# Routing stage of a two-layer decoder step: which engine splits the expert tiles, how many are issued per routing step, and where the softmax exponentials stand

## The chip, the cores and the metric

The kernel runs on one core of a Trainium2 chip. A core has TensorE (PE, matrix products; PEld is its weight load), VectorE (DVE), ScalarE (ACT), GpSimd (POOL) and SyncE (SP, which issues most transfers). Each engine works through its own instructions strictly in order and waits for others only by semaphores. The metric is the device time of one execution in microseconds (us), lower is better.

## The reference, cut to what matters

Two layers; in each, three token mixers are merged, then a PEER expert mixer follows. Only the expert mixer matters here:

```
q  = (x @ p_wq).reshape(T, 8 heads, 2 halves, 128)
sc = einsum('thjc,hjkc->thjk', q, p_keys)            # 128 keys in each half
s, i  = top_k(sc, 16)
cand  = s[:,:,0,:,None] + s[:,:,1,None,:]            # 16 x 16 sums
cidx  = i[:,:,0,:,None]*128 + i[:,:,1,None,:]
top_s, pos = top_k(cand.reshape(T, 8, 256), 16)
eidx  = take_along_axis(cidx, pos);  g = softmax(top_s)
act   = gelu(u[eidx] . x) * g
out   = sum_k act[k] * v[eidx[k]]                    # 16384 experts
```

There are 256 prompt tokens and 32 sample tokens (8 sequences of 4), and 1024 channels.

## The kernel before, in words

For the prompt tokens the kernel does not gather experts. It multiplies all 16384 rows of `u` with the tokens, as 128 *expert tiles* of 128 rows (`u_tile`), takes the Gelu, multiplies with gate weights that are zero for experts not chosen, and then multiplies with all of `v` (`experts`). For the 32 sample tokens it gathers rows.

All products are made from float32 values split in two: `split` writes the rounded high part with a ScalarE copy (line 209) and the low part with a subtraction (line 210) on VectorE, or on GpSimd where `eng` is given. `proj` loads a 512 KB weight tile, splits it, and issues 24 matrix products in one PSUM bank: 16 with the high weights (lines 253 and 254) and 8 with the low ones (line 256). So the low part is wanted only after the first 16. There are two such banks (`ps_pj`), three raw buffers (`NRAW`) and four buffers for the split halves (`NHI`), that is two tiles' worth.

`peer` runs a layer's expert mixer in three stages. **Routing**: the generator `routing` issues the query projections, the scores, the maxima and the index lookups, and after each of its `yield`s `peer` adds `RU[phase]` to a due count and issues one more expert tile when the count asks for it. What a `yield` yields is the phase: 0 beside the score maxima (36 yields, 16 of them ahead of the second half of the query projections), 1 beside the maxima of the candidate sums (18), 2 beside the lookups (26). **Gate weights**: `gate_weights` for 8 tokens at a time, with the remaining expert tiles between. **Experts**: the products with `v`.

In the routing, one call of `top16` is a chain of five VectorE operations (maximum of 8, index, replace, maximum of 8, index). Tokens come in three segments `s` of 128, 128 and 32. In phase 2, each segment begins with its softmax (subtraction of the maximum, `Exp` on ScalarE, sum, reciprocal, product), then index arithmetic, then for each of two words the lookups `eq`, `eq`, `res` in pairs of heads. Then PE turns the results and the digits of the keys go to `pd`, `pu` and `pg`, which the gate weights read.

In the mixers and in the experts stage, the order of each engine's instructions is the program's. In the routing and the gate stage it is not: a scheduler orders them when the program is built. It plays out a timeline with its own durations, and puts next on an engine the instruction that is earliest in the program among those it takes as ready. That order is then fixed. When an operation takes longer on the chip than in that timeline, everything behind it on its engine waits. `Exp` and `Gelu` are in different function tables of ScalarE, so each change between them loads a table.

The routing's temporary tiles (`tk`) and the second part of the Gelu outputs (`WB`, 28 KB per partition) take the same memory one after the other, and the tiles of the gate stage (`gw`) lie behind `WB`.

Of the kernel before, what the change touches and what calls it, by code (L numbers as in the profile page):

```python
# [7 lines left out]
F32 = mybir.dt.float32  # L8
# [7 lines left out]
AF = mybir.ActivationFunctionType  # L16
OP = mybir.AluOpType
AX = mybir.AxisListType
# [4 lines left out]
TP = 256  # L23
# [21 lines left out]
NGB = 4  # L45
XPRE = (3, 7)
PEX = 6
RU = (0.25, 0.5, 1.05)

GS = 2.0 ** 15  # L50
RATE = (24, 30, 18, 6, 24, 14, 12)
# [14 lines left out]
def bc(ap, shape):  # L66
    return ap.to_broadcast(shape)


class Kernel:  # L70
# [1223 lines left out]
    def peer(self):  # L1294
        tc = self.tc
        with tc.tile_pool(name="pk", bufs=1) as self.pk:
            with tc.tile_pool(name="wa", bufs=1) as wa:
# [3 lines left out]
                with tc.tile_pool(name="tk", bufs=1) as self.tk:  # L1301
                    due = 0.0
                    for self.phase in self.routing():
                        due += RU[self.phase]
                        if self.jdone < min(J1, int(due)):
# [32 lines left out]
    def routing(self):  # L1338
        ve, ac, sy, pe, L, I, tk = self.ve, self.ac, self.sy, self.pe, self.L, self.I, self.tk
# [3 lines left out]
        def top16(src, n, v, i, w):  # L1343
            ve.max(v[:, 0:8], src)
            ve.max_index(i[:, 0:8], v[:, 0:8], src)
            tmp = tk.tile([128, w], F32, tag="tmp", name="tmp", bufs=2)
            ve.match_replace(tmp, v[:, 0:8], src, -3.0e38)  # L1347
            ve.max(v[:, 8:16], tmp)
            ve.max_index(i[:, 8:16], v[:, 8:16], tmp)

        pss = self.ps_rc("pss").rearrange("p (m k) -> p m k", k=128)
        for grp in range(2):
# [5 lines left out]
            for t in range(2):  # L1358
                for half in range(2):
                    p = self.ps_rc("psc").rearrange("p (m k) -> p m k", k=128)  # L1360
# [4 lines left out]
            for s2 in range(2):  # L1365
                s = 2 * grp + s2
# [3 lines left out]
            for t, half, p in banks:  # L1370
                for m in range(4):
                    h, j = divmod(8 * grp + 4 * half + m, 2)
# [6 lines left out]
        picks = []  # L1379
        for s in range(3):  # L1380
            H = 8 if s < 2 else 2
            v, ix = val[s], idx[s]
            cand = tk.tile([128, H, 80], F32, tag="cand", name="cand")
            s0, s1 = v[:, :, 0], v[:, :, 1]
            a0 = 0
            for g, (na, nbb) in enumerate(((1, 16), (1, 16), (2, 8), (4, 4), (8, 2))):
                ve.tensor_tensor(cand[:, :, 16 * g:16 * g + 16].rearrange("p h (a b) -> p h a b", b=nbb),  # L1387
                                 bc(s0[:, :, a0:a0 + na].unsqueeze(3), [128, H, na, nbb]),
                                 bc(s1[:, :, None, 0:nbb], [128, H, na, nbb]), op=OP.add)
                a0 += na  # L1390
            top = tk.tile([128, H, 16], F32, name=f"top{s}")
            pos = tk.tile([128, H, 16], U32, name=f"pos{s}")
            for h in range(H):
                top16(cand[:, h], 128, top[:, h], pos[:, h], 80)
                yield 1
            picks.append((top, pos))
        for s in range(3):
            H, ix = 8 if s < 2 else 2, idx[s]

            (tops, pos), top = picks[s], tk.tile([128, H, 16], F32, tag="tope", name="tope")  # L1400
            ve.tensor_tensor(top, tops, bc(tops[:, :, 0:1], [128, H, 16]), op=OP.subtract)
            ac.activation(top, top, AF.Exp)
            z = tk.tile([128, H], F32, tag="z", name="z")
            ve.tensor_reduce(z, top, axis=AX.X, op=OP.add)
            ve.reciprocal(z, z)
            gd = self.sg if s == 2 else top
            ve.tensor_tensor(gd.rearrange("p (h r) -> p h r", r=16) if s == 2 else gd, top,
                             bc(z.unsqueeze(2), [128, H, 16]), op=OP.mult)
            yield 2

            it = lambda n: tk.tile([128, H, 16], I32, tag="it", name=n, bufs=5)
            p32 = pos.bitcast(I32)
            gq, r = it("gq"), it("r")
            ve.tensor_scalar(gq, p32, 4, None, op0=OP.logical_shift_right)
            ve.tensor_scalar(r, p32, 15, None, op0=OP.bitwise_and)
            sh = it("sh")
            ve.tensor_scalar(sh, gq, -1.0, 5.0, op0=OP.mult, op1=OP.add)
            t1 = it("t1")
            ve.tensor_tensor(t1, r, sh, op=OP.logical_shift_right)
            t2 = it("t2")  # L1420
            ve.tensor_tensor(t2, t1, sh, op=OP.logical_shift_left)
            bq = r
            ve.tensor_tensor(bq, r, t2, op=OP.subtract)
            ve.tensor_tensor(t2, bc(self.one_i[:, 0:1].unsqueeze(2), [128, H, 16]), gq, op=OP.logical_shift_left)
            ve.tensor_scalar(t2, t2, 1, None, op0=OP.logical_shift_right)
            aq = t1
            ve.tensor_tensor(aq, t1, t2, op=OP.add)
            yield 2
            out = []
            for w_, place in ((0, aq), (1, bq)):  # L1430
                pf = tk.tile([128, H, 16], BF16, tag="pf", name="pf")
                ve.tensor_copy(pf, place)
                kf = tk.tile([128, H, 16], BF16, tag="kf", name="kf")
                ve.tensor_copy(kf, ix[:, :, w_])
                res = tk.tile([128, H, 16], F32, tag=f"res{w_}", name=f"res{w_}")
                for h0 in range(0, H, 2):
                    eq = tk.tile([128, 2, 16, 16], BF16, tag="eq", name="eq", bufs=2)
                    ve.tensor_tensor(eq, bc(pf[:, h0:h0 + 2].unsqueeze(3), [128, 2, 16, 16]),
                                     bc(self.iota16[:, None, None, :], [128, 2, 16, 16]), op=OP.is_equal)
                    ve.tensor_tensor(eq, eq, bc(kf[:, h0:h0 + 2].unsqueeze(2), [128, 2, 16, 16]), op=OP.mult)  # L1440
                    ve.tensor_reduce(res[:, h0:h0 + 2], eq, axis=AX.X, op=OP.add)
                    yield 2
                out.append(res)
            if s < 2:
                tt = slice(s * 128, (s + 1) * 128)
                keys = tk.tile([128, 2, 128], F32, tag="keys", name="keys")
                ki = tk.tile([128, 2, 128], I32, tag="ki", name="ki")
                for src, dst, scale in ((out[0], keys[:, 0], 1.0), (out[1], keys[:, 1], 1.0), (top, self.pg[:, 0, tt], GS)):
                    pt = self.ps_rc("ptk")[:, :128]
                    pe.transpose(pt, src.rearrange("p h r -> p (h r)"), self.ident)  # L1450
                    ac.activation(dst, pt, AF.Copy, scale=scale)
                ve.scalar_tensor_tensor(self.pg[:, 1, tt], pt, GS, self.pg[:, 0, tt], op0=OP.mult, op1=OP.subtract)
                ve.tensor_copy(ki, keys)
                ve.tensor_scalar(ki, ki, 15, None, op0=OP.bitwise_and)
                ve.tensor_copy(self.pu[:, :, tt], ki)
                ve.tensor_tensor(self.pd[:, :, tt], keys, self.pu[:, :, tt], op=OP.subtract)
                yield 2
            else:
                f = lambda x: x.rearrange("p h r -> p (h r)")
                for dst, hi, lo in ((self.se, out[0], out[1]), (self.sv, out[1], out[0])):  # L1460
                    ve.scalar_tensor_tensor(dst, f(hi), 128.0, f(lo), op0=OP.mult, op1=OP.add)
                    if L:
                        ve.tensor_scalar(dst, dst, float(L * 16384), None, op0=OP.add)


    def u_tile(self):
        ac, j, t = self.ac, self.jdone, self.tdone
        self.jdone += 1
        ps = self.proj(self.I["ut"][self.L, j], "pu", TP, self.gp if self.phase in (0, 1) else None)
        w = self.slot(j)  # L1470
        if t < TP:
            ac.activation(w[:, t:], ps[:, t:], AF.Gelu)  # L1472
        if t:
            ge = self.gw.tile([128, TP], F32, tag="ge", name="ge", bufs=2)
            ac.activation(ge[:, :t], ps[:, :t], AF.Gelu)
            self.ve.tensor_tensor(w[:, :t], w[:, :t], ge[:, :t], op=OP.mult)
# [366 lines left out]
```

## Time and profile before

| | |
|---|---|
| median of 3 runs | 2542.75 us (2541.96 to 2546.72) |
| the profiled execution | 2553.09 us |
| its span, first to last instruction | 2551.3 us |
| PE busy | 2457.7 us (96%) |
| PEld busy | 2235.0 us (88%) |
| DVE busy | 1935.7 us (76%) |
| ACT busy | 1328.5 us (52%) |
| POOL busy | 269.9 us (11%) |
| granted TensorE clock, mean | 0.979 |

A row names the engine, the line of the kernel, and the tiles as written<-read. "Idle before" is what the engine stood still ahead of an instruction, with the one that released it. Instructions on VectorE and matrix products on PE overlap a little with the next, so the step from start to start is shorter than the duration. The profiled execution's routing of layer 0 lies between 427 and 634 us, that of layer 1 between 1695 and 1902 us.

### The profile page before, as it was taken

To read this page: it belongs to the slowest core of one execution; us is meant where nothing else is said; L and a number is where in the kernel's file an instruction comes from. 1 tells how busy PE (TensorE), PEld (TensorE's weight loads), DVE (VectorE), ACT (ScalarE), POOL (GpSimd) and SP (SyncE) were. 2 spreads that over 40 slices of the span, in tenths; PEclk is the share of its full clock that TensorE was granted. 3 is DMA by queue.
4 is the path that set the end of the run, shared out by engine and by line. 5 is a ranking of instruction groups with operands and counts; after the bars stand their busy time and mean duration, and the time that the engine had idled before them with its cause. 6 is when DMAs were issued, how large, how long until landed. Compare 5 with 4: busy or idle time off the path is not lost. (4 is left out here: it accounts for less than half of the span.)

```text
span 2551.3 us, 45304 instructions
## 1 busy us (share of the span) xinstructions
PE 2457.7 (96%) x17014; PEld 2235.0 (88%) x17014; DVE 1935.7 (76%) x4156; ACT 1328.5 (52%) x2675; POOL 269.9 (11%) x270
## 2 busy tenths in 40 slices
PE   8998998989999999999999999989899999999998
PEld 8987897989999988777789888889899999878886
DVE  7667666699778868888676776767997787688885
ACT  6444765445554444444564457653455544444544
POOL 0000100240000012222000001003300000122210
PEclk9999999999999999999999989999999999999999
DMA  4422543546545568888544225434455455688883
GB/s 163 136 92 82 183 143 111 166 143 190 167 163 166 162 216 304 313 305 300 167 134 137 83 88 188 146 111 163 157 183 166 161 164 165 234 308 311 311 281 132
DMA packets 132028, 465.10 MB, mean 182 GB/s; under 512 B 15360, under 2 KB 17536, under 8 KB 131808
## 3 DMA queue, kind: packets, MB, share of 16 engines
q1 hardware_dynamic: 109728, 385.14, 45.4%
q0 software_dynamic: 22080, 77.06, 9.0%
q8 instruction: 134, 2.20, 0.3%
q14 instruction: 86, 0.70, 0.1%
HBM read 451.32 MB, written 10.82 MB: 181 GB/s over the span
## 5 line engine op out<-in xcount | busy, mean ns | idle before, releaser
L210 DVE TENSOR_TENSOR hl<-raw,hl 128x1024 fp32r<-128x1024 f32 (+1 forms) x842 | 844.8, 1008 | 393.3 <-ACT hl L209 382.5
L209 ACT ACTIVATE hl<-raw 128x1024 fp32r<-128x1024 f32 (+1 forms) x880 | 778.2, 888 | 461.4 <-PE pu L254 144.6
L1555 PE MATMUL acc<-hl,wh 128*128 128x512 f32 x2048 | 648.3, 396 | 2.6 <-ACT hl L209 1.4
L253 PE MATMUL pu<-hh,hl 128*128 128x256 f32 x2048 | 504.5, 287 | 12.4 <-ACT WA L1472 12.2
L254 PE MATMUL pu<-hl 128*128 128x256 f32 x2048 | 494.9, 280 | 0.0
L1555 PEld LDWEIGHTS acc<-hl,wh 128*128 128x128 f32 x2048 | 384.7, 188 | 100.5 <-ACT hl L209 4.9
L1555 PE MATMUL acc<-hl,wl 128*128 128x512 f32 x1024 | 404.9, 395 | 0.0
L253 PEld LDWEIGHTS pu<-hh,hl 128*128 128x128 f32 x2048 | 388.2, 190 | 14.1 <-ACT WA L1472 13.3
L254 PEld LDWEIGHTS pu<-hl 128*128 128x128 f32 x2048 | 387.8, 189 | 0.0
L326 PE MATMUL pz<-xl,hl 128*128 128x288 f32 x1008 | 325.0, 322 | 0.6 <-DVE xl L1663 0.3
L324 PE MATMUL pz<-xh,hl 128*128 128x288 f32 x1008 | 308.5, 306 | 11.8 <-ACT xh L209 6.8
L328 PE MATMUL pz<-xh,hl 128*128 128x288 f32 x1008 | 306.7, 304 | 0.0
L256 PE MATMUL pu<-hh,hl 128*128 128x256 f32 x2048 | 284.8, 282 | 2.3 <-DVE hl L210 2.3
L256 PEld LDWEIGHTS pu<-hh,hl 128*128 128x128 f32 x2048 | 260.0, 189 | 3.1 <-DVE hl L210 3.0
L1555 PEld LDWEIGHTS acc<-hl,wl 128*128 128x128 f32 x1024 | 192.5, 188 | 45.7
L209 ACT ACTIVATE wh<-WA 128x256 fp32r<-128x256 f32 x200 | 83.6, 418 | 269.1 <-PE acc L1555 266.7
L326 PEld LDWEIGHTS pz<-xl,hl 128*128 128x128 f32 x1008 | 197.4, 196 | 16.7 <-issue 11.5
L324 PEld LDWEIGHTS pz<-xh,hl 128*128 128x128 f32 x1008 | 197.6, 196 | 14.5 <-ACT xh L209 7.4
L328 PEld LDWEIGHTS pz<-xh,hl 128*128 128x128 f32 x1008 | 198.4, 197 | 3.7 <-issue 2.7
L1676 POOL DMA_INDIRECT gbuf<-in_u,se x64 | 61.7, 964 | 963.3 <-PE pu L256 701.0
L210 DVE TENSOR_TENSOR wl<-WA,wh 128x256 fp32r<-128x256 f32 x200 | 84.3, 422 | 48.4 <-ACT wh L209 48.2
L210 POOL TENSOR_TENSOR hl<-raw,hl 128x1024 fp32r<-128x1024 f32 (+1 forms) x38 | 89.6, 2357 | 188.2 <-ACT hl L209 165.6
(584 smaller groups left out, 3366.0 us busy)
## 6 DMA issues: line engine op xcount, KB each, us to landing
raw<-in_ut SPq DMA_DIRECT2D x256, 512.0 KB, 3.5
raw<-in_v SPq DMA_DIRECT2D x256, 512.0 KB, 4.7
raw<-in_win SPq DMA_DIRECT2D x126, 512.0 KB, 3.6
raw<-in_wq SPq DMA_DIRECT2D x32, 512.0 KB, 3.5
raw<-in_wbr SPq DMA_DIRECT2D x24, 512.0 KB, 3.5
raw<-in_wout SPq DMA_DIRECT2D x16, 512.0 KB, 3.6
CS<-in_C SPq DMA_DIRECT2D x16, 256.0 KB, 3.9
out_sC<-CS POOLq DMA_DIRECT2D x16, 256.0 KB, 2.8
```

What stands on the lines that cost most here:

```text
L209: self.ac.activation(hi, r, AF.Copy)
L210: (eng or self.ve).tensor_tensor(lo, r, hi.bitcast(F32), op=OP.subtract)
L253: self.pe.matmul(ps, wh[k], self.xh[:, k, :n], start=(k == 0), stop=False)
L254: self.pe.matmul(ps, wh[k], self.xl[:, k, :n], start=False, stop=False)
L256: self.pe.matmul(ps, wl[k], self.xh[:, k, :n], start=False, stop=(k == 7))
L324: self.pe.matmul(ps, hi[:, m], xh, start=(first and m == 0), stop=False)
L326: self.pe.matmul(ps, hi[:, m], xl, start=False, stop=False)
L328: self.pe.matmul(ps, lo[:, m], xh, start=False, stop=last)
L1555: pe.matmul(acc[t][d], lhs[:, 128 * t:128 * t + 128], rhs, start=False, stop=last and n == 2, skip_group_check=True)
L1676: self.gp.indirect_dma_start(out=g, out_offset=None, in_=src, in_offset=bass.IndirectOffsetOnAxis(ap=ix[:, r:r + 1], axis=0))
```

## The change

Three things are changed. The rates `RU` at which expert tiles are issued: more in phase 0, the same in phase 1, fewer in phase 2. The engine of the low parts' subtraction for expert tiles: GpSimd in phase 0 alone, where it was phases 0 and 1. The softmax: the subtraction stands with the candidate maxima (phase 1), for each segment in a tile `ex` of its own; the three `Exp` stand together after the first word's lookups of segment 0, each pinned behind what is already issued on ScalarE; the sum, the reciprocal and the product come after the segment's lookups. The `yield 2` behind the old softmax is gone, so phase 2 has 23 yields.

```diff
-RU = (0.25, 0.5, 1.05)
+RU = (0.42, 0.5, 0.9)
...
-            picks.append((top, pos))
+            ex = tk.tile([128, H, 16], F32, name=f"ex{s}")
+            ve.tensor_tensor(ex, top, bc(top[:, :, 0:1], [128, H, 16]), op=OP.subtract)
+            picks.append((pos, ex))
         for s in range(3):
             H, ix = 8 if s < 2 else 2, idx[s]
-
-            (tops, pos), top = picks[s], tk.tile([128, H, 16], F32, tag="tope", name="tope")
-            ve.tensor_tensor(top, tops, bc(tops[:, :, 0:1], [128, H, 16]), op=OP.subtract)
-            ac.activation(top, top, AF.Exp)
-            z = tk.tile([128, H], F32, tag="z", name="z")
-            ve.tensor_reduce(z, top, axis=AX.X, op=OP.add)
-            ve.reciprocal(z, z)
-            gd = self.sg if s == 2 else top
-            ve.tensor_tensor(gd.rearrange("p (h r) -> p h r", r=16) if s == 2 else gd, top,
-                             bc(z.unsqueeze(2), [128, H, 16]), op=OP.mult)
-            yield 2
+            pos, top = picks[s]
...
                 out.append(res)
+
+                if s == w_ == 0:
+                    for _, ex in picks:
+                        self.tc.keep_in_program_order(ac.activation(ex, ex, AF.Exp))
+
+            z = tk.tile([128, H], F32, tag="z", name="z")
+            ve.tensor_reduce(z, top, axis=AX.X, op=OP.add)
+            ve.reciprocal(z, z)
+            gd = self.sg if s == 2 else top
+            ve.tensor_tensor(gd.rearrange("p (h r) -> p h r", r=16) if s == 2 else gd, top,
+                             bc(z.unsqueeze(2), [128, H, 16]), op=OP.mult)
...
-        ps = self.proj(self.I["ut"][self.L, j], "pu", TP, self.gp if self.phase in (0, 1) else None)
+        ps = self.proj(self.I["ut"][self.L, j], "pu", TP, self.gp if self.phase == 0 else None)
```

## Rows read from the trace of the kernel before

**Rows 1.** Page, part 1: busy us (share of the span) and instructions of each engine.
```profile
PE 2457.7 (96%) x17014; PEld 2235.0 (88%) x17014; DVE 1935.7 (76%) x4156; ACT 1328.5 (52%) x2675; POOL 269.9 (11%) x270
```
**Rows 2.** Waits of PE, 427 to 640 us: who for whom, total us, times, longest.
```profile
PE pu L253 <- ACT WA L1472: 6.1, 1, 6.1
...
PE pu L256 <- DVE hl L210: 1.0, 1, 1.0
```
**Rows 3.** Timeline of PE at the long wait, both layers: start, us, instructions [idle before].
```profile
533.77 1.11 PE L256 MATMUL pu<-hh,hl 128*128 128x256 f32 x8
...
536.58 1.11 PE L256 MATMUL pu<-hh,hl 128*128 128x256 f32 x8
543.81 0.58 PE L253 MATMUL pu<-hh,hl 128*128 128x256 f32 x1 [6.12 <-ACT WA L1472]
...
547.40 1.55 PE L256 MATMUL pu<-hh,hl 128*128 128x256 f32 x8
...
1811.48 0.58 PE L253 MATMUL pu<-hh,hl 128*128 128x256 f32 x1 [6.12 <-ACT WA L1472]
```
**Rows 4.** Timeline of ACT around the same wait, layer 0.
```profile
535.09 1.28 ACT L1402 ACT_TABLE_LOAD   x1
541.75 0.31 ACT L1402 ACTIVATE tope<-tope 128x128 f32<-128x128 f32 x1 [5.38 <-DVE tope L1401]
542.08 1.28 ACT L1472 ACT_TABLE_LOAD   x1
543.38 0.38 ACT L1472 ACTIVATE WA<-pu 128x256 f32<-128x256 f32 x1
```
**Rows 5.** Timeline of DVE: three long operations, one of usual length, the awaited subtraction.
```profile
513.60 1.95 DVE L1387 TENSOR_TENSOR cand<-val 128x128 f32<-128x128 f32 x1
...
516.15 1.79 DVE L1434 CAST kf<-idx 128x128 bf16<-128x128 uint32 x1
...
541.25 0.27 DVE L1387 TENSOR_TENSOR cand<-val 128x128 f32<-128x128 f32 x1
541.44 0.28 DVE L1401 TENSOR_TENSOR tope<-top 128x128 f32<-128x128 f32 x1
...
549.53 2.13 DVE L1425 TENSOR_SCALAR t<-t 128x128 int32<-128x128 int32 x1
```
**Rows 6.** Timeline of POOL at the same times: the expert tiles' low parts.
```profile
512.64 5.22 POOL L210 TENSOR_TENSOR hl<-raw,hl 128x1024 fp32r<-128x1024 f32 x2 [0.41 <-ACT hl L209]
...
549.08 2.50 POOL L210 TENSOR_TENSOR hl<-raw,hl 128x1024 fp32r<-128x1024 f32 x1 [1.92 <-ACT hl L209]
```
**Rows 7.** Timelines of PE and DVE at the first expert tile that DVE splits.
```profile
550.65 1.11 PE L256 MATMUL pu<-hh,hl 128*128 128x256 f32 x8
...
556.28 1.22 PE L256 MATMUL pu<-hh,hl 128*128 128x256 f32 x8
555.01 1.21 DVE L210 TENSOR_TENSOR hl<-raw,hl 128x1024 fp32r<-128x1024 f32 x1
```
**Rows 8.** Busy us (count) of PE, PEld, DVE, ACT, POOL; PE clock; DMA.
```profile
460.00:505.00 45.00, 45.00 (x359) 44.04 (x358) 30.94 (x151) 18.42 (x27) 12.07 (x6) 1.00 0.51 164
505.00:537.70 32.70, 32.69 (x281) 32.16 (x279) 32.70 (x193) 14.33 (x20) 24.40 (x10) 1.00 0.53 177
537.70:549.00 11.30, 5.19 (x26) 5.19 (x27) 11.30 (x77) 4.28 (x7) 2.38 (x1) 0.70 0.20 59
549.00:634.00 85.00, 83.88 (x717) 83.16 (x716) 82.20 (x202) 45.74 (x70) 2.50 (x1) 1.00 0.57 179
```
**Rows 9.** Groups of DVE's instructions by line, 504.9 to 634.8 us: busy, mean ns | idle.
```profile
L210 DVE TENSOR_TENSOR hl<-raw,hl 128x1024 fp32r<-128x1024 f32 x30 | 36.4, 1216 | 3.7 <-ACT hl L209 3.4 <-issue 0.3
...
L1515 DVE TENSOR_TENSOR oj<-dgd,dones 128x1024 int32<-128x1024 int32 x3 | 3.6, 1214 | 0.0
```
**Rows 10.** Timeline of DVE: first digits of the gate stage; the routing's last lookup.
```profile
599.19 0.35 DVE L1490 TENSOR_TENSOR dhi<-iota_hi,pd 128x128 f16<-128x128 f16 x2
...
632.99 0.18 DVE L1461 SCALAR_TENSOR_TENSOR se<-res,res 128x32 int32<-128x32 f32 x1
```

## The prediction

> **What bounds the kernel now.** I read the page first. PE is busy for 96% of the span and nothing else comes near [rows 1], so a saving must be time in which PE stands still or runs slowly, and work taken from another engine counts only where PE waits for it. Next, the waits of PE over the routing of layer 0: apart from the start of the stage, which the change leaves alone, there is one wait of 6.1 us for a Gelu (line 1472) and one of 1.0 us for a low half from VectorE (line 210) [rows 2]. Layer 1 has the same long wait, 6.12 us [rows 3].
>
> Then the timelines. An expert tile's last products normally end 2.81 us after those of the tile before (536.58 after 533.77, equal durations). Around the wait they end 11.26 us later (548.95 after 537.69) [rows 3]. So the wait costs 11.26 - 2.81 = 8.45 us: 6.12 of idling and some 2.2 because the tile that follows runs with products of 0.4 us each. The stretch around it has a mean granted clock of 0.70 where its neighbours have 1.00 [rows 8]: after the idle time the lower of the two levels (1.2 instead of 2.4 GHz) was granted for about one tile.
>
> Why PE waited: there are two PSUM banks for expert tiles, and ScalarE did not empty them. It had loaded the table of `Exp` at 535.09, ahead of a Gelu whose products were finished, and stood 5.38 us until VectorE had written the softmax's subtraction at 541.44 to 541.72. Only after a second table load came the Gelu, at 543.38 [rows 4, 5]. The order was fixed at build with that subtraction taken as ready by about 535; on the chip VectorE was some 6.5 us behind. It was not idle: it is busy for all of 505 to 549 [rows 8]. A good part of the delay is visible in it. Sums of candidates and casts that normally take about 0.27 us take 1.8 to 2.1 us, and end when a GpSimd subtraction ends [rows 5, 6]. There are five such operations in each layer, about 1.7 us too long each (the three shown: 1.68, 1.6, 1.9); three lie ahead of 521 us, two behind 545 us. The maxima beside them are not prolonged.
>
> **The change part by part.** *Counts.* Before: 36 x 0.25 + 18 x 0.5 + 26 x 1.05 = 45.3, so 45 expert tiles in the routing, 18 of them split by GpSimd, 4 ahead of the second query projections. After: 15.12 + 9 + 23 x 0.9 = 44.8, so 44, of which GpSimd splits 15 and 6 lie ahead of the second projections. All 128 are issued in any case, one more in the gate stage, so PE's own work stays as it is.
>
> *The exponentials.* They are now pinned behind the Gelu of tile 28 (24.12 + 5 x 0.9 = 28.6), where the old one stood ahead of that of tile 14. The 8.45 us per layer at the old place go, 16.9 us in all. What comes in their place: one table load, three exponentials and a load back, 1.28 + 0.9 + 1.30 = 3.5 us in which ScalarE does nothing else, if it need not wait. The old block ran from 535.09 to 543.38, 8.3 us, for 6.1 us of PE's idling [rows 3, 4], so some 2 us of a block are hidden by the two banks. That leaves 1.3 us per layer if they stand in one piece, 0 if a copy goes between; I take 1. The four table loads saved per layer (5.1 us of ScalarE) lie beside PE's work and are worth nothing. Bounds: -0 and +3.3, the latter if VectorE is as late with segment 2's subtraction as it is below with a split.
>
> The Trainium skill, ScalarE: Activation LUTs, section "What ACT_TABLE_LOAD costs", gives 2.66 us for a switch, a drain of 1.38 us beside the load of 1.28 us. Here the Gelu starts 1.30 us after the load does [rows 4], so no drain shows; by the page the new block would be 2.7 us longer and this term 3.7 us instead of 1.
>
> *GpSimd in phase 0 alone.* Nine tiles of phase 1 move to VectorE, and six new ones of phase 0 go to GpSimd: VectorE splits 29 instead of 27. The two blocked operations behind 545 us go (3.4 us of VectorE), the three ahead of 521 us stay (5.1 us), since they lie beside phase 0's tiles now as before. So VectorE still falls behind its planned order by 5 to 6.5 us while GpSimd splits. Before, tiles 10 to 18 did not ask VectorE for anything and PE ran on until the exponential. Now tile 16 asks it. The cover: the buffer of a low half is free when the tile two ahead has ended (551.76), and the low half is wanted 4.5 us later (556.28), of which 1.21 us is the subtraction, so VectorE may be 3.1 us late; at the first such tile of before it was just that [rows 7]. What is left is 5 to 6.5 less 3.1, 2 to 3.4 us per layer; I take 3. Bounds: 0, if the scheduler's order has room there, and 6.5, if none of the cover is left. Behind it, waits of the kind that before shows (1.0 us [rows 2]) stay: 1.3 us per layer.
>
> *Fewer tiles beside the lookups, more ahead.* With two more tiles ahead of the second projections, the second scores come 2 x 2.81 = 5.6 us later. VectorE has no work then (it idles 14 of the 45 us from 460 to 505 [rows 8]), while PE is ahead by the two tiles. From there to the last lookup, VectorE must do: busy 126.2 us from 505 to 634 [rows 8], less 28 splits of 1.21 us, 34 [rows 9], less about 8 of gate work done early (three `oj` of 1.21 us, three `oi` of half that, their digits [rows 9, 10]), less 8.6 of blocking, which is 75.6. In the new kernel: 75.6 + 5.1 + 29 x 1.21 = 116 us, from 510.6 to 626. PE needs 38 x 2.81 = 107 us for its tiles, from 512 to 619. So VectorE ends 7 us behind PE where before both ended together (last lookup at 632.99 [rows 10]). PE can pass this with tiles of the gate stage: two banks and two `ge` buffers hold four, 11 us. I cost it at nothing; without that cover it is 7 us and more (the third rival).
>
> *The small rest* (the subtraction in another tile, the sum and product later) are the same instructions; 0.
>
> *Sum.* Before, per layer: 8.45 + 1.0 = 9.4. After: 1 + 3 + 1.3 = 5.3. The gain is 4.1 per layer, 8.2 us for both. The profiled execution would go from 2553.1 to 2544.9; it is 10.3 us above the median of the runs, so I take the difference from the median: 2542.75 - 8.2 = 2534.5 us.
>
> **The rivals.** *A, the wait goes and nothing takes its place.* For it: VectorE shows little idle time but also few late splits from 560 on, though it is busy for 82.2 of 85 us [rows 8], so the fixed order can absorb a delay; and phase 0 now takes 36 maxima beside 15 tiles, at nearly PE's pace. Against it: the three blocked operations stay. It gives 16.9 to 18.8 us less: 2524 to 2526.
>
> *B, the wait moves.* The delay of VectorE, not the place of the `Exp`, is the cause; the first splits of phase 1 and the pinned exponentials inherit it. The delay is 6.5 us at least; less one cover, plus 3.5 for the block and later waits, it costs 7.5 to 9.5 per layer. It gives 2542.75 within 4 us: 2539 to 2544. For it: VectorE is full from 505 on [rows 8]. Against it: a wait in small pieces need not lower the clock (after the 1.0 us wait products have their usual length), and two of five blocks are gone.
>
> *C, slower: VectorE's tail holds the gate stage.* The place is the end of the routing. The routing's temporary tiles grow: `ex` takes 512 + 512 + 128 bytes per partition and `tope` gives back 512, which by my count brings them from 28448 to 29088 bytes, over the 28672 of `WB`, and so under the first tile of the gate stage, `dhi`. Before, the digits began at 599.19, 34 us ahead of the last lookup [rows 10]; then they must wait for the key tiles of segment 1. If the scheduler lets PE have no tile beyond the 44th meanwhile, PE stands from 619 to 626 and on through 4 to 6 us of gate work that was done early before: 12 to 13 us, with 2.3 for the other waits some 15 per layer against 9.4. That is +5 per layer: about 2553. It decides from the point at which fewer than two extra tiles are let in: each gives PE 2.81 us for 1.21 of VectorE.
>
> The Trainium skill, GPSIMD Engine Reference, section "Key points", says that GpSimd shares its SBUF interfaces with VectorE and collides with instructions of two SBUF inputs. The rows agree for the candidate sums [rows 5, 6]. No row shows a VectorE split, which also has two SBUF inputs, beside a GpSimd one; by the page tile 16's, beside tile 15's, could lose up to 2.4 us, and the sum would be 2.4 per layer worse.
>
> **How the numbers follow.** The forecast, 5 to 12 us less, 0.42; A 0.20; B 0.23; C 0.15. The time is the forecast's: 2534.5 us. The range reaches to A's 2524 and over B's 2544 to 2546; it leaves out most of C and a little below A. A change under 0.2% (5.1 us) can hardly be told from none here. Faster by more: the forecast and A, 0.62. Within: B, 0.23. Slower: C, 0.15.
>
> **What would show it.** In the new trace: no 6 us wait of PE for a Gelu near 537 and 1805 us, and a granted clock of 1.00 there; one load of the `Exp` table per layer; 15 GpSimd splits per layer; three long VectorE operations per layer and none after GpSimd stops; a wait of PE for `hl` from VectorE of 2 to 3.4 us at the first tile of phase 1; at most 1 us of waiting around the exponentials; no PE gap between routing and gate stage. The prediction is wrong if the `Exp` still stands on VectorE for over 3 us, if the waits for `hl` add up to over 6 us per layer, or if PE idles where the gate stage begins.

## The result, and the profile after

The changed kernel is slower. Its median is 2562.95 us (2557.55 to 2571.68) beside 2546.14 us for the kernel before (8 runs of each); the ratio is **1.0063, 95% interval 1.0046 to 1.0079**, or 12 to 20 us. I had forecast 2534.5 us, within 2524 to 2546: the sign was wrong. The profiled execution took 2563.68 us (span 2561.9 us, mean granted clock 0.979, as before).

The busy times (columns as in [rows 1]) say little: PE has the same work, and the span has grown beside it.

```profile
PE 2459.6 (96%) x17014; PEld 2240.3 (87%) x17014; DVE 1938.0 (76%) x4162; ACT 1314.1 (51%) x2667; POOL 250.4 (10%) x264
```

The waits of PE in the routing of layer 0, 420 to 660 us (who for whom: total us, times, longest), answer to [rows 2]. The first line stands at the first VectorE split, the second and third at the end of the routing, the last at the exponentials.

```profile
PE pu L256 <- DVE hl L210: 3.6, 1, 3.6
PE pu L253 <- ACT ge L1478: 3.4, 1, 3.4
PE pg L1527 <- DVE oj L1518: 3.2, 1, 3.2
PE pu L253 <- ACT WA L1475: 2.0, 1, 2.0
```

The single wait of 6.1 us [rows 2] is gone. Four waits of 2.0 to 3.6 us have taken its place, 12.2 us in all. In layer 1 they are `hl` 4.0, `ge` 3.4 and `WA` 2.0 us, and none for `oj`.

**The first VectorE split.** Timelines of PE and DVE (columns as in [rows 3]), layer 0:

```profile
529.13 1.11 PE L256 MATMUL pu<-hh,hl 128*128 128x256 f32 x8
535.71 2.07 PE L256 MATMUL pu<-hh,hl 128*128 128x256 f32 x8 [3.61 <-DVE hl L210]
541.00 1.30 PE L256 MATMUL pu<-hh,hl 128*128 128x256 f32 x8
...
511.55 1.96 DVE L1387 TENSOR_TENSOR cand<-val 128x128 f32<-128x128 f32 x1
514.10 2.03 DVE L1426 CAST kf<-idx 128x128 bf16<-128x128 uint32 x1
516.32 2.67 DVE L1387 TENSOR_TENSOR cand<-val 128x128 f32<-128x128 f32 x2
534.45 1.20 DVE L210 TENSOR_TENSOR hl<-raw,hl 128x1024 fp32r<-128x1024 f32 x1
```

Two tiles end at 537.78 and 542.30, 7.54 and 4.52 us after the one before them, where 2.81 is usual [rows 3]. So the wait costs 6.4 us (5.4 in layer 1), not the 3.6 us of idling: behind it the lower of the two clock levels (1.2 GHz) was granted for a while again (the mean is 0.73 in the first of the stretches below), as behind the old wait in [rows 8].

**The exponentials.** Timeline of ACT, then of PE, around them:

```profile
575.14 0.39 ACT L1475 ACTIVATE WA<-pu 128x256 f32<-128x256 f32 x1 [1.07 <-PE pu L256]
575.54 1.28 ACT L1439 ACT_TABLE_LOAD   x1
576.83 0.63 ACT L1439 ACTIVATE ex<-ex 128x128 f32<-128x128 f32 x3
577.37 1.04 ACT L209 ACTIVATE hl<-raw 128x1024 fp32r<-128x1024 f32 x1
578.32 0.25 ACT L1454 ACTIVATE keys<-ptk 128x128 f32<-128x128 f32 x1
578.59 1.28 ACT L1475 ACT_TABLE_LOAD   x1
579.88 0.38 ACT L1475 ACTIVATE WA<-pu 128x256 f32<-128x256 f32 x1
...
574.00 1.10 PE L256 MATMUL pu<-hh,hl 128*128 128x256 f32 x8
575.20 1.21 PE L256 MATMUL pu<-hh,hl 128*128 128x256 f32 x8
...
578.01 0.28 PE L254 MATMUL pu<-hl 128*128 128x256 f32 x1
580.32 0.39 PE L253 MATMUL pu<-hh,hl 128*128 128x256 f32 x1 [2.03 <-ACT WA L1475]
```

One table load for `Exp`, no wait of ACT for VectorE: this part does what it says. But PE works on two tiles in turn here, and both are finished within 1.3 us (575.10 and 576.41). The block stands between their two Gelus and takes 4.3 us, since a copy of a split and an eviction are caught between its loads. The first Gelu has emptied one bank, and PE works in it until 578.29; then it needs the other, whose Gelu is 3.5 us late, and waits 2.0 us. In layer 1 the wait is the same, but behind it the lower clock level was granted (products of 0.41 instead of 0.28 us; layer 0 kept 1.00). Columns as in [rows 8]:

```profile
1860.00:1870.00 10.00, 8.91 (x62) 8.91 (x63) 7.12 (x16) 4.65 (x7) 0.00 (x0) 0.83 0.52 160
```

**The end of the routing.** Timelines of ACT, DVE and PE. The Gelu at 621.36 is the 44th, the last that writes all 256 tokens without `ge`:

```profile
621.36 0.37 ACT L1475 ACTIVATE WA<-pu 128x256 f32<-128x256 f32 x1
627.21 0.36 ACT L1475 ACTIVATE WA<-pu 128x248 f32<-128x248 f32 x1
630.30 0.24 ACT L1478 ACTIVATE ge<-pu 128x8 f32<-128x8 f32 x2 [2.73 <-DVE pd L1459]
...
629.79 0.42 DVE L1459 TENSOR_TENSOR pd<-keys,pu 128x256 f16<-128x256 f32 x1
630.24 0.36 DVE L1493 TENSOR_TENSOR dhi<-iota_hi,pd 128x128 f16<-128x128 f16 x2
...
626.05 1.11 PE L256 MATMUL pu<-hh,hl 128*128 128x256 f32 x8
630.53 0.58 PE L253 MATMUL pu<-hh,hl 128*128 128x256 f32 x1 [3.37 <-ACT ge L1478]
...
642.79 1.08 PE L1527 MATMUL pg<-oj,oi 128*128 128x128 f16 x16 [3.15 <-DVE oj L1518]
```

Two tiles of the gate stage, the 45th and 46th, get through and fill the two banks. Their `ge` may be written only after the last key tile (`pd`, until 630.21). PE stands for it, then stands again for the first gate weights, whose digits `dhi` began behind `pd` too (before, they began at 599.19 [rows 10]). Counted from the first product of the query projections, that `pd` is done 209.8 us into the stage (211.9 in layer 1), 6.2 and 8.5 us later than before. Busy times in stretches (columns as in [rows 8]): the first split, the routing's last tiles, its end, where the clock falls too.

```profile
530.00:540.00 10.00, 6.39 (x39) 6.19 (x38) 10.00 (x64) 2.15 (x4) 0.00 (x0) 0.73 0.22 68
...
612.00:627.00 15.00, 15.00 (x130) 14.95 (x128) 13.36 (x27) 8.07 (x14) 0.00 (x0) 1.00 0.67 200
627.00:650.00 23.00, 16.32 (x145) 15.90 (x144) 21.87 (x60) 6.99 (x21) 0.00 (x0) 0.85 0.28 91
```

**Where the time went, by stage.** I measure, in each layer's timeline, the time from the first product of the query projections to the end of the Gelu of the 28th, 44th and 50th expert tile, and to the first product with `v`, and take it from that of the kernel before. Positive is ahead (us, layer 0 / layer 1; the kernel before: 159.0 / 158.7, 204.5 / 204.3, 222.8 / 222.6, 477.4 / 477.2). The kernels of the experiments are in the same table; "tiles" is how many expert tiles the routing issues.

| kernel | tiles | at 28 | at 44 | at 50 | at `v` | ratio to before (95%) |
|---|---|---|---|---|---|---|
| changed | 44 | 3.9 / 3.1 | 3.2 / 0.9 | -9.5 / -6.3 | -7.8 / -5.6 | 1.0063 (1.0046 to 1.0079) |
| e1_ex_in_qT | 44 | 3.9 / 3.7 | 1.0 / 2.4 | -5.4 / -4.0 | -4.7 / -3.3 | 1.0047 (1.0035 to 1.006) |
| e2_before_pad | 44 | -0.5 / -0.1 | 0.9 / 1.4 | 0.2 / 0.6 | 0.0 / 0.5 | 0.9993 (0.9979 to 1.0006) |
| e3_softmax_only | 41 | 1.0 / 2.4 | -0.1 / 1.4 | -0.1 / 1.6 | 1.3 / 2.8 | 0.9991 (0.9975 to 1.0007) |
| e4_rates_only | 47 | 3.9 / 3.7 | 5.4 / 5.2 | 3.3 / 3.1 | 3.7 / 3.4 | 0.998 (0.9964 to 0.9995) |
| e6_rate_up | 47 | 4.1 / 3.9 | 5.1 / 5.0 | 3.7 / 3.6 | 3.9 / 3.9 | 0.9976 (0.9958 to 0.9994) |
| e7_exp_apart | 47 | 3.5 / 3.6 | 4.0 / 4.3 | 2.5 / 2.7 | 3.0 / 3.3 | 0.9961 (0.9941 to 0.998) |
| e8_rates_pinned_adds | 47 | 8.0 / 7.6 | 5.9 / 5.6 | 7.0 / 6.7 | 6.8 / 6.5 | 0.9953 (0.9934 to 0.9971) |
| e9_rate_up_only | 47 | 4.3 / 3.7 | 5.9 / 5.4 | 7.1 / 6.6 | 3.1 / 2.6 | 0.9976 (0.9961 to 0.9991) |
| e10_apart_pinned | 47 | 7.5 / 7.5 | 5.6 / 5.7 | 5.6 / 5.7 | 5.7 / 5.9 | 0.9957 (0.994 to 0.9974) |

The changed kernel is ahead up to the 44th tile, by somewhat less than I had summed, and loses 12.7 and 7.2 us between the 44th and the 50th. A part of these two numbers is order: 65 and 49 of the gate weights' products stand there, 29 in the kernel before, and 16 of them take about 1 us. The two layers' -7.8 and -5.6 make 13.4 us, inside the measured 12 to 20. The last two columns agree within the interval for every kernel but e1 (8.0 us by the stage, 9 to 15 by the ratio), so the stage explains the time.

What was open was the cause at the end of the routing: the grown temporary tiles, which put the first gate tiles behind `pd`; the number of tiles PE has left when VectorE finishes; or the softmax itself.

### The profile page after: what moved, and what is told of

Read it like the earlier page. It is cut to its first block, busy times and chain, and to the rows that moved or that the text cites. A ratio compares the mean times of both kernels' runs of the same rounds, so it can differ in the third digit from the quotient of the medians.

```text
span 2561.9 us, 45294 instructions
## 1 busy us (share of the span) xinstructions
PE 2459.6 (96%) x17014; PEld 2240.3 (87%) x17014; DVE 1938.0 (76%) x4162; ACT 1314.1 (51%) x2667; POOL 250.4 (10%) x264
## 5 line engine op out<-in xcount | busy, mean ns | idle before, releaser
L210 POOL TENSOR_TENSOR hl<-raw,hl 128x1024 fp32r<-128x1024 f32 (+1 forms) x32 | 74.6, 2332 | 170.3 <-ACT hl L209 147.9
```

What stands on the lines that cost most here:

```text
L210: (eng or self.ve).tensor_tensor(lo, r, hi.bitcast(F32), op=OP.subtract)
```

## The experiments

### e1_ex_in_qT: the changed kernel without the growth of its temporary tiles

```diff
         picks = []
+        exs = tk.tile([128, 18, 16], F32, tag="qT", name="ex")
...
-            ex = tk.tile([128, H, 16], F32, name=f"ex{s}")
+            ex = exs[:, 8 * s:8 * s + H]
```

> The changed kernel with one thing undone: the three ex tiles take the memory of qT, which is dead by then, so the routing's temporary tiles do not grow and the gate stage's first tiles no longer lie over key tiles. Theory M (memory): the gate stage's digits can again be written before the routing ends; the waits of PE for ge (3.4 us per layer) and oj (3.2 us) and the slow tiles behind them go. Of the 12.7 and 7.2 us that the changed kernel loses between expert tiles 44 and 50, about 10 and 6 come back: some 2 to 6 us faster than the kernel before, ratio 0.998 to 1.000. Theory V (VectorE's tail): two tiles more ahead of the second scores and fewer beside the lookups leave VectorE late whatever the memory; it stays at the changed kernel's ratio, 1.004 to 1.008.

**Measured:** 2562.19 us, ratio 1.0047 (1.0035 to 1.006). The `ge` no longer waits for `pd`, and the stage gains 3.1 and 2.3 us over the changed kernel. But it is still slower than before. VectorE now does gate work ahead of the routing's last lookups, so the last key tile comes later (645.66 instead of 629.79), and a copy on ACT into `WB`, which takes the memory of the routing's tiles, waits for it. PE still stands 2.9 us for a `ge`, in both layers. Timelines of DVE and ACT, and PE's wait:

```profile
645.66 0.43 DVE L1460 TENSOR_TENSOR pd<-keys,pu 128x256 f16<-128x256 f32 x1
...
646.18 0.73 ACT L1537 ACTIVATE WB<-pg 128x112 f32<-128x112 f32 x4 [3.13 <-DVE pd L1460]
...
PE pu L253 <- ACT ge L1479: 2.9, 1, 2.9
```

**What follows:** the memory decides what waits for VectorE's tail, not whether something does. By the stage 5.4 of 13.4 us went with the growth, and the two ratios' intervals overlap; the larger part of the loss stays.

### e2_before_pad: the kernel before with as much growth

```diff
-            z = tk.tile([128, H], F32, tag="z", name="z")
+            z = tk.tile([128, 8 + 160], F32, tag="z", name="z")[:, :H]
```

> The kernel before with 640 bytes per partition of padding in the tile z, so that the routing's tiles end where those of the changed kernel do; no work is changed. Theory M: the digits move behind the last key tile, PE waits at the start of the gate stage as in the changed kernel, and the time rises by 6 to 18 us, ratio 1.002 to 1.007. Theory V: memory plays no part, ratio 1.000 within 0.001.

**Measured:** ratio 0.9993 (0.9979 to 1.0006). The first digits begin at 624.0 instead of 599.19 [rows 10], yet the table's row is that of the kernel before within 1.4 us. **What follows:** 25 us of delay of the early gate work cost nothing where PE's routing tiles reach as far as VectorE's tail. The growth alone, without the other edits, is not the cause.

### e3_softmax_only: the new softmax with the old rates and the old use of GpSimd

The kernel is that of e1 with these two lines as before:

```diff
-RU = (0.42, 0.5, 0.9)
+RU = (0.25, 0.5, 1.05)
...
-        ps = self.proj(self.I["ut"][self.L, j], "pu", TP, self.gp if self.phase == 0 else None)
+        ps = self.proj(self.I["ut"][self.L, j], "pu", TP, self.gp if self.phase in (0, 1) else None)
```

> The kernel before with the softmax alone moved (ex in the memory of qT); the rates and GpSimd's phases are those of before. If the place of the Exp was the cause of the long wait, the 6.1 us wait and the slow tile go in both layers: 12 to 17 us faster, ratio 0.993 to 0.995. If VectorE's delay is the cause and only moves, PE waits elsewhere (first VectorE split, new Exp) for about as long: ratio 0.998 to 1.001.

**Measured:** ratio 0.9991 (0.9975 to 1.0007). The wait for the Gelu is gone, and at the first VectorE split this stands in its place (timeline of PE, layer 0; 5.1 us in layer 1):

```profile
540.12 1.11 PE L256 MATMUL pu<-hh,hl 128*128 128x256 f32 x8
550.44 2.08 PE L256 MATMUL pu<-hh,hl 128*128 128x256 f32 x8 [7.34 <-DVE hl L210]
```

**What follows:** VectorE is late, and the old `Exp` was only where PE met it. Moving the `Exp` moves the wait to the next thing that PE wants of VectorE: rival B's mechanism. This kernel issues only 41 tiles in the routing, and PE waits nowhere at its end: VectorE, with 23 splits in the routing instead of 29, is done with the last `pd` 205.5 and 203.8 us into the stage, and the gate stage's first tiles get through. So it is not the count of tiles by itself that decides, but whether PE's tiles reach as far as VectorE's tail.

### e4_rates_only: the new rates and GpSimd in phase 0 alone, the old softmax

The kernel before with the two lines of e3 the other way round. The old softmax keeps its `yield 2`, so phase 2 has 26 yields and the routing issues 47 tiles.

> The kernel before with the rates and the GpSimd phases alone changed; the softmax is the old one. The Exp of segment 0 may still be placed ahead of a Gelu, and the first VectorE split of phase 1 now meets a VectorE that is 5 to 6.5 us late. If the delay passes on to whatever asks VectorE first: a wait for hl of about 3.5 us per layer, little left for the Exp to wait, ratio 0.998 to 1.002. If both waits add: ratio 1.002 to 1.005.

**Measured:** ratio 0.998 (0.9964 to 0.9995). The 6.1 us wait is gone here too, though the `Exp` stands where it stood: ACT comes to it later and finds the subtraction done (table load at 547.20, `Exp` at 548.50, no wait). What is left is 3.6 us for `hl` and 0.6 us for `ge` in each layer. **What follows:** the rates and the engine alone make the kernel a little faster, and the end of the routing costs little (1.7 and 1.8 us of lead between the 44th tile and `v`). What the new softmax brings beside its place is three yields fewer, hence three tiles fewer.

### e6_rate_up: the kernel of e1 with 47 tiles

```diff
-RU = (0.42, 0.5, 0.9)
+RU = (0.42, 0.5, 1.03)
```

> The changed kernel with ex in the memory of qT (as in the run before, which alone gave a ratio of 1.0047) and 1.03 instead of 0.9 expert tiles per step of phase 2: 47 tiles are issued in the routing as where only the rates were changed, instead of 44. Theory T: PE runs out of routing tiles before VectorE ends its lookups, and the gate stage is held by that tail; three tiles more cover it, 4.3 us per layer come back between tiles 44 and 50: ratio 1.0005 to 1.002. Theory X: only the joint block of the exponentials costs; nothing comes back, ratio 1.0035 to 1.006.

**Measured:** 2542.29 us, ratio 0.9976 (0.9958 to 0.9994), against 1.0047 for e1: 0.71%, or 18 us, for one number. The wait for `ge` at the end of the routing and the 2.0 us at the exponentials are gone; 3.6 us for `hl` (4.0 in layer 1) and 0.4 us for `WA` stay. **What follows:** with these rates and this use of GpSimd, 44 tiles are too few, at least without the growth.

### e9_rate_up_only: the changed kernel with 47 tiles, growth and all

The same one-number edit, on the changed kernel itself.

> The changed kernel with one number altered: phase 2's rate is 1.03 instead of 0.9, so 15.1 + 9 + 23 x 1.03 = 47.8, 47 expert tiles in the routing instead of 44; the softmax and its tiles stay as changed, memory growth included. Nothing of the computation is left out. Theory S (tile supply: PE runs out of routing tiles while VectorE finishes the lookups): the loss goes although the memory grows; ratio to before 0.996 to 1.000, 2540 to 2549 us; no wait of PE for `oj` or for a late `ge` of more than 1 us, and tile 50 ends 3 us earlier than before. Theory M (the grown temporary tiles hold `dhi` and with it the gate stage): most of the loss stays; ratio 1.003 to 1.006, 2557 to 2563 us, with `dhi` still behind the last key tile and a wait of 3 us for `oj`.

**Measured:** 2543.95 us, ratio 0.9976 (0.9961 to 0.9991), where the changed kernel has 1.0063 (0.87% less, 22 us). Waits of PE in layer 0, then the end of the routing on ACT and DVE:

```profile
PE pu L256 <- DVE hl L210: 4.0, 2, 3.6
PE pg L1527 <- DVE oj L1518: 1.2, 1, 1.2
...
PE pu L253 <- ACT ge L1478: 0.3, 1, 0.3
```

```profile
624.12 0.36 ACT L1475 ACTIVATE WA<-pu 128x256 f32<-128x256 f32 x1
626.93 0.36 ACT L1475 ACTIVATE WA<-pu 128x248 f32<-128x248 f32 x1
627.19 0.17 ACT L1478 ACTIVATE ge<-pu 128x8 f32<-128x8 f32 x1
...
625.39 0.42 DVE L1459 TENSOR_TENSOR pd<-keys,pu 128x256 f16<-128x256 f32 x1
625.84 0.36 DVE L1493 TENSOR_TENSOR dhi<-iota_hi,pd 128x128 f16<-128x128 f16 x2
```

The digits still stand behind `pd`, as in the changed kernel, but the last tile without `ge` ends at 624.48, 1.3 us ahead of `pd`'s end (625.81); in the changed kernel it ends 8.5 us ahead (621.73 and 630.21), in the kernel before 0.9 us behind it (632.08 and 631.22). Three tiles are 8.4 us.

The wait at the exponentials has gone too. The higher rate shifted the pinned block by one Gelu, to behind both of a pair, so that both banks were empty and PE had work for all of its 4.2 us (timeline of ACT):

```profile
571.54 0.38 ACT L1475 ACTIVATE WA<-pu 128x256 f32<-128x256 f32 x1 [1.05 <-PE pu L256]
...
572.93 0.39 ACT L1475 ACTIVATE WA<-pu 128x256 f32<-128x256 f32 x1
573.33 1.28 ACT L1439 ACT_TABLE_LOAD   x1
...
576.23 1.28 ACT L1475 ACT_TABLE_LOAD   x1
577.55 0.38 ACT L1475 ACTIVATE WA<-pu 128x256 f32<-128x256 f32 x1
```

From the 28th to the 44th tile it takes 43.9 us in both layers, the changed kernel 46.2 and 47.8: so the block cost 2.3 and 3.9 us there, the latter with the lower clock.

**What follows:** the theory of the tile supply stands, that of the memory falls; of the 19.1 us that the stage gains, 6.2 are the block's. The wait for `oj` is 0.2 to 0.4 us longer than the theory had allowed, and part of the lead is lost behind the 50th tile (7.1 to 3.1 us). Some of that is order again: here no product of the gate weights stands ahead of the 50th tile, in the kernel before 46, some 3 us. The wait for `oj` is all that the list shows of the late digits; e6, without the growth, has the same ratio.

### e7_exp_apart: the kernel of e6 with one `Exp` in each segment

```diff
-                if s == w_ == 0:
-                    for _, ex in picks:
-                        self.tc.keep_in_program_order(ac.activation(ex, ex, AF.Exp))
+                if w_ == 0:
+                    self.tc.keep_in_program_order(ac.activation(top, top, AF.Exp))
```

> As the run with 1.03, with each segment's Exp at its own segment, still pinned, behind the first word's lookups, so three blocks of a load, one Exp and a load instead of a joint one. Theory X: the joint block of 4.4 us on ScalarE (with a copy and an eviction caught between the loads) meets two expert tiles that end almost together, so the two banks cover nothing; blocks 1 us shorter are covered better: the wait for WA of 2.0 us and the slow tile behind it go, 4 us per layer, ratio 0.997 to 0.999 if the tail is cured too. If the number of table loads counts, it is as slow as the run with the joint block or slower by up to 3 us.

**Measured:** ratio 0.9961 (0.9941 to 0.998); its interval overlaps that of e6, and the stage's table shows no gain over it. **What follows:** together or apart can't be told here; four more table loads in each layer [rows 4] lie beside PE's work, as I had assumed.

### e8_rates_pinned_adds: the kernel of e4, with operations kept away from GpSimd's splits

The sums of candidates and the first cast of segment 0 are held in program order on VectorE, so that they can't be taken early, between the maxima and beside GpSimd.

```diff
-                ve.tensor_tensor(cand[:, :, 16 * g:16 * g + 16].rearrange("p h (a b) -> p h a b", b=nbb),
+                add = ve.tensor_tensor(cand[:, :, 16 * g:16 * g + 16].rearrange("p h (a b) -> p h a b", b=nbb),
...
+                if s == 0:
+                    self.tc.keep_in_program_order(add)
...
-                ve.tensor_copy(kf, ix[:, :, w_])
+                cast = ve.tensor_copy(kf, ix[:, :, w_])
+                if s == w_ == 0:
+                    self.tc.keep_in_program_order(cast)
```

> The run with the rates and the GpSimd phases alone, with segment 0's candidate sums and first cast pinned in program order on VectorE, so that they no longer stand beside GpSimd's subtractions. If these blocked operations (three per layer, 1.5 to 2.4 us too long each) make VectorE late, no operation of 1.8 us stands beside GpSimd, the wait of 3.6 us for the first low half of phase 1 falls to 0 to 1 us and the slow tile behind it goes: 6 us per layer, ratio 0.993 to 0.996. If VectorE is late for its own load, the wait stays and the ratio is 0.998 as there.

**Measured:** 2535.82 us, ratio 0.9953 (0.9934 to 0.9971): the lowest ratio of all, though the intervals of the other kernels with 47 tiles overlap it. Waits of PE in layer 0, and on DVE and POOL the one prolonged operation that is left:

```profile
PE pu L253 <- ACT WA L1476: 1.6, 3, 0.6
PE pu L256 <- DVE hl L210: 1.0, 2, 0.6
```

```profile
525.55 3.29 DVE L1387 TENSOR_TENSOR cand<-val 128x128 f32<-128x128 f32 x5
...
525.91 2.57 POOL L210 TENSOR_TENSOR hl<-raw,hl 128x1024 fp32r<-128x1024 f32 x1 [0.41 <-ACT hl L209]
```

All five sums are done 0.36 us after GpSimd's last subtraction ends (528.84 and 528.48). The wait for `hl` falls from 3.6 to 1.0 us, and the 28th tile ends 4.1 and 3.9 us earlier than in e4. **What follows:** e4 has three such operations ahead of its first split, of 1.96, 2.03 and 2.49 us, some 5.7 us too long in all; here there is one, of 2.49 us, 2.2 too long. The 3.5 us less are enough for the 2.6 us by which the wait falls, so the blocked operations account for VectorE's lateness at the first split. The pins also change the order of other work on VectorE, and no run separates the two.

### e10_apart_pinned: both cures

The kernel of e7 with the pins of e8.

> The kernel with the `Exp` apart and rate 1.03 (0.996), with segment 0's sums of candidates and its first cast held in program order on VectorE, as in the pinned kernel on the old softmax. Nothing is left out. Theory D (blocked operations beside GpSimd's subtractions make VectorE late, and the first splits of phase 1 pay): the wait for `hl` of 3.6 us per layer falls to 1 us or less, tile 28 ends 4 us earlier than in the kernel without the pins, and the gain stays to the end of the stage: 3 to 4 us per layer, ratio 0.992 to 0.994, 2529 to 2535 us. Rival (the pins only move the lateness, since VectorE has the same work): the `hl` wait shrinks and another wait of PE grows by as much behind tile 28; ratio 0.995 to 0.997, 2537 to 2542 us.

**Measured:** ratio 0.9957 (0.994 to 0.9974). The wait for `hl` falls to 1.5 us and the 28th tile is 4 us earlier than in e7, as the theory of the blocked operations has it; at the first product with `v` 2.7 and 2.6 us of it are left. But the ratio lies in the other theory's band, and the intervals of e7, e8 and e10 overlap. So the gain in the stage is shown by the traces, and what of it reaches the end is not told apart.

## Why the prediction was wrong, point by point

**What bounds the kernel: right.** The time is PE's waits in the routing; with the slow tiles behind them they make up the measured difference, as the table by stage shows.

**Counts: half wrong.** 44 tiles after, 15 of them on GpSimd, were right, and so were the three prolonged operations per layer with none behind GpSimd's last split. Before there were 44 too, not 45: one tile at most is issued for each yield, so a rate of 1.05 can't give more than the 26 yields, and 18 + 26 = 44. The miscount changed no term, but it hid what the rate of 0.9 does: with 26 yields it gives 47 tiles, with 23 it gives 44.

**The wait at the `Exp`: right in size, half right in cause.** VectorE's delay was named, but the place of the `Exp` was taken as what makes PE pay for it. The 8.45 us per layer went. But e4 loses it with the `Exp` where it was, and e3 moves the `Exp` and only trades the wait for one of 7.3 us. The order of the softmax was no cause by itself.

**The new block of exponentials: mis-sized.** 1 us taken, 2.3 and 3.9 us measured, the second beyond the bound of 3.3. The part that the banks hide was right: 2.3 us of the 4.3 here. The block itself was too short in the sum, 3.5 us: a copy between its parts was counted as cover (0 us), but it lengthens the block when it is caught between the loads. In layer 1 the lower clock came on top. In e9, where both banks are empty when it begins, the block costs nothing. The Gelu starts 1.29 us after its table load (578.59 to 579.88). By the Trainium skill, ScalarE: Activation LUTs, section "What ACT_TABLE_LOAD costs", a switch takes 2.66 us; the trace shows half of that here as well, so the page's longer switch is not why the term was too small.

**The first split: mechanism right, size wrong.** 3 us taken, 6.4 and 5.4 measured. The wait of 3.6 us lay just above the expected 2 to 3.4; the rest, 2.8 and 1.8 us, is the lower clock behind it. I had counted that for the old wait and not for the new one, and rival B's argument, that small waits need not lower the clock, was read from a wait of 1.0 us.

**Fewer tiles beside the lookups: the step that failed.** I found VectorE 7 us behind PE at the end of the routing and costed it at nothing, because "two banks and two `ge` buffers hold four, 11 us". VectorE was 8.5 us behind in both layers, so that number was good. The cover was not: it held two tiles, 5.6 us, because the `ge` buffers could not be written before the last key tile. Behind it came the gate weights, begun late, with a second wait in layer 0. Between the 44th and the 50th tile it costs 12.7 and 7.2 us against the kernel before, which did with 44 tiles: there VectorE was done 6.2 and 8.5 us earlier in the stage, and PE's 44th tile 3.2 and 0.9 us later. Three more tiles (e9) undo the loss.

**Rival C was the case**, given 0.15: the place was right, and 2553 us as the time was near (1.0063 times 2542.75 is 2558.8 us). Of the 12 to 13 us of standing 6.5 came in layer 0 and 3.4 in layer 1; the 12.7 us of layer 0 have slow products and the order of the gate's products in them. Its condition, fewer than two extra tiles, was not met: two got through, and that was not enough. The memory does put `ge` and the digits behind `pd`, but e2 shows that costs nothing by itself, e1 that the larger part of the loss outlives it, and e9 that three more routing tiles undo the loss with the memory as it is. Why the scheduler places VectorE's gate work ahead of the last lookups in e1, I have not traced.

**The sum.** I forecast 8.2 us less; by the stages it is 13.4 us more, a miss of 21.6 us. Up to the 44th tile the lead is 4.1 us for both layers instead of 8.2. The end of the routing costs 19.9 us instead of nothing, of which 2.4 us come back later: 4.1 + 19.9 - 2.4 = 21.6. That the lead at the 44th tile is short by 4.1 us alone, though the split and the block cost 10 us more than I took, is in part because the later waits for `hl`, 1.3 us per layer, hardly came (0.4 us in layer 1), and in part order: in the kernel before 17 products of the gate weights stand ahead of the 44th tile, in the changed one none (in e2, where there are none either, the tiles from the 28th to the 44th take 1.4 us less per layer than before). About 1 us of it is not traced. With 47 tiles (e9) the change saves 5.7 us in the stage, near the sum: there the first split costs 5.4 and 6.4 us and the block nothing that can be seen.

The Trainium skill, GPSIMD Engine Reference, section "Key points", made me price a VectorE split beside a GpSimd one. In the changed kernel the first such split begins at 534.45, after GpSimd's last of the routing has ended (527.29), and in no other trace do the two overlap, so no run here shows it.

## What to carry to other kernels

When an edit takes steps out of a loop that also paces another engine's work, recount that work at the loop's end: here a removed `yield` at the new rate left PE with 44 tiles instead of 47, with more work on VectorE beside them, and that cost more than the wait the edit removed. A cover is worth only what may be used before the thing waited for; so trace each buffer that should hold work (here the `ge`) back to what frees it, and count how many of them are empty when the stall begins (one empty bank hid 2.3 us of a block on ScalarE, two hid all of its 4.2 us). And a wait that ends in VectorE's lateness moves with the edit until the lateness itself is taken away.

## What the runs showed of the hardware that I had not expected

A VectorE operation that meets a GpSimd subtraction can end with it, and the order decides how often that is paid. In the changed kernel three such meetings take 1.96, 2.03 and, for two operations together, 2.67 us (a single one of these operations normally takes about 0.27 us [rows 5]). With the same operations put together, five sums pay one meeting, 3.29 us in e8.

Waits that look alike in the list need not cost alike, because the clock behind them differs. In layer 0 of the changed kernel the lower level was granted behind the wait of 3.6 us for `hl`, after PE had been busy for the whole 30 us ahead of it, and not behind that of 2.0 us at the exponentials (a mean of 1.00 over 575 to 585 us). In layer 1 it was granted behind that same wait of 2.0 us too (0.83 over 1860 to 1870 us). By the tiles' ends the wait for `hl` cost 6.4 and 5.4 us in the two layers, that at the exponentials 2.3 and 3.9 us.
